# A decoder step on one core: sums over a head as two single-pass products of a split operand, and six instead of seven pairs of weight halves

## The chip, the core and the metric

The kernel runs on one core of a Trainium2 chip. The core has five engines that work side by side, each through its own list of instructions in a fixed order: TensorE (PE, matrix products into PSUM), VectorE (DVE), ScalarE (ACT), GpSimd (POOL) and SyncE (SP), which here issues the transfers. An instruction that waits holds back everything behind it on its engine. The metric is the time of one execution on the device in microseconds, the median of several runs.

## The reference

One layer of a hybrid decoder, for 256 prompt tokens and 8 decode tokens: 264 columns, with 2048 features each. A half-step FFN, a mixing stage with attention and RWKV-7 heads side by side, a second FFN, a final norm. What concerns the change are two sums over the 64 features of an RWKV head: the bonus, and the norm of each head's output.

```python
def swiglu(x, wg, wu, wd):
    return (jax.nn.silu(x @ wg) * (x @ wu)) @ wd
...
    S, y = wkv_scan(wkv0, r, logw, k, v, kk, a)
    mean = jnp.mean(y, axis=-1, keepdims=True)
    var = jnp.mean((y - mean) ** 2, axis=-1, keepdims=True)
```

The normalised y gets a weight and a bias per feature, then the bonus is added (the head's sum of r times k times a weight, times v), and the whole is multiplied by a gate. All inputs and outputs are float32.

## The kernel before

Activations lie features first: a tile is 128 features by 264 columns. A pair of RWKV heads fills the 128 rows, so there are eight pairs p = 0 to 7, in four batches of two.

**GEMMs.** A big product is made of single-pass matmuls (type float32r). Weight and activation are each split in two halves: hi, the value rounded by a cast, and lo, what is left. `gemm` (L143) does three matmuls per 128 features: hi by hi, hi by lo, lo by hi. Weights come from memory as raw tiles, four blocks of 128 wide; `chunk` (L125) casts one to hi on ScalarE (L136) and subtracts on VectorE to get lo (through `tt`, L58). A chunk so feeds 12 matmuls. NRAW = 7 raw buffers and NHL = 7 pairs of halves lie in rings. Small products use full fp32 operands.

**Stages.** The first FFN runs from 0 to about 700 us, the mixing stage to about 1107, the second FFN to the end. In the mixing stage 38 tiles of the input projection (`win`) are made one after another, then the output projection in three passes over the mixed tiles (`PASS`): tiles 0 to 3, then 8 to 11 with 4 and 5, then 6, 7 and 12 to 15. Tiles 0 to 7 are RWKV pairs, 8 to 15 attention.

**Order.** All that is not GEMM in the mixing stage is written as tasks, Python generators. `tick` takes each live task one step on, up to its next `yield`, and is called once a chunk of the GEMM. `pause(n)` lets n ticks go by, so that a product is written only when its operand has had time to be made. `drain` ticks without GEMM until the named tasks have ended. The order of each engine is settled when the program is built, from the written order, priorities and a modelled timeline. The tasks here are `prep` (one pair: decay, keys, bonus), `chain` (one batch: the scan over four chunks of 64 tokens, then `gnorm` per pair, then gate and `mixed[p]`), `attend` (one tile of attention), and `dec_load(p)` and `dec_attend(p)` (the decode tokens' attention, tiles 8 to 11 for p = 0 and 12 to 15 for p = 1). `dec_load(1)` begins only when the last batch's chain and `dec_attend(0)` have ended, and `dec_attend(1)` must end before pass 2 begins, since tiles 12 to 15 belong to it. The steps of `dec_attend`: scores, softmax, transposes (L871) and their copy out of PSUM (L872), products with the values, two multiply-adds, transposes back (L884), copies (L887, L889). Pass 2 then splits its tiles in halves (L939).

**The two sums.** C holds constants: `bo` is the block matrix of ones for two heads, `cm` the identity minus the mean over a head. The bonus product takes `rk` (280 columns: 264 and two columns for each of the 8 decode tokens). In `gnorm` the product with `cm` gives y minus its mean, and the one with `bo` on its square the variance:

```python
                yield from pause(PW[2])
                bps = mp()
                mm(bps[:, :T + 2 * NB], bo, rk)
...
                yp = mp()
                mm(yp[:, :T], cm, y)
                r = tmp()
                act(r, yp[:, :T], AF.Square)
                yield from pause(PW[3])
                vp = mp()
                mm(vp[:, :T], bo, r)
```

PW = (2, 1, 3, 2, 2) holds the lengths of the pauses. `chain` drives its batch's `gnorm` tasks for PW[3] + 1 = 3 ticks.

## Time and profile before

| | us |
|---|---|
| median of 3 runs | 1849.22 (1845.97 to 1851.04) |
| the profiled execution, a run of its own | 1846.21 |
| its span, first to last instruction | 1844.4 |
| granted TensorE clock, mean | 0.998 |
| first FFN, mixing, second FFN | about 700, 407, 737 |

Rows of the profile name an engine, a line of the kernel, an operation, the tile written and the tiles read, with shapes as partitions by elements. PEld is TensorE's loading of weights, which lies beside its products. A row of waits gives the engine that waits, the tile that it was to write, the engine and tile that it waited for, the total, the number and the longest wait. A row of the chain of waits gives a start, a length and the work in it. L58 and L61 are the lines of the helpers `tt` and `stt`, L74 that of `mm`.

### The profile page before, as it was taken

To read this page: it belongs to the slowest core of one execution; us is meant where nothing else is said; L and a number is where in the kernel's file an instruction comes from. 1 tells how busy PE (TensorE), PEld (TensorE's weight loads), DVE (VectorE), ACT (ScalarE), POOL (GpSimd) and SP (SyncE) were. 2 spreads that over 40 slices of the span, in tenths; PEclk is the share of its full clock that TensorE was granted. 3 is DMA by queue.
4 is the path that set the end of the run, shared out by engine and by line. 5 is a ranking of instruction groups with operands and counts; after the bars stand their busy time and mean duration, and the time that the engine had idled before them with its cause. 6 is when DMAs were issued, how large, how long until landed. Compare 5 with 4: busy or idle time off the path is not lost.

```text
span 1844.4 us, 46192 instructions
## 1 busy us (share of the span) xinstructions
PE 1821.4 (99%) x17212; PEld 1792.4 (97%) x17212; DVE 1311.4 (71%) x2613; ACT 1068.6 (58%) x2134; POOL 258.4 (14%) x389
## 2 busy tenths in 40 slices
PE   9999999999999999999998999999999999999998
PEld 9999999999999999998987899999999999999997
DVE  6966665656656577799888677876766676667765
ACT  6645555455554557777767766654545555455555
POOL 0401101010010122122111200220101001010012
PEclk9999999999999999999999999999999999999999
DMA  8666666666666677555666446666666666666664
GB/s 270 191 202 213 196 210 205 201 199 188 204 190 201 196 201 244 174 169 146 174 174 183 143 127 220 185 201 189 203 207 208 193 211 203 203 208 193 216 189 136
DMA packets 226465, 358.25 MB, mean 194 GB/s; under 512 B 38440, under 2 KB 82112, under 8 KB 226240
## 3 DMA queue, kind: packets, MB, share of 16 engines
q1 hardware_dynamic: 220352, 349.20, 62.9%
q10 hardware_dynamic: 5888, 6.11, 1.1%
q8 instruction: 135, 2.21, 0.5%
q14 instruction: 90, 0.74, 0.1%
HBM read 347.06 MB, written 10.22 MB: 194 GB/s over the span
## 4 chain that ended last, share of the span: by engine, by line
PE 91%; DVE 3%; DMA 3%; issue 1%; ACT 1%; POOL 0%; SPq 0%; POOLq 0%; ACTq 0%; DVEq 0%
PE acc L74 84%; PE m L74 6%; DVE lo L58 1%; DMA raw<-in_gu 1%; DMA raw<-in_win 0%; DVE Xt L58 0%; DVE st L58 0%; DMA X<-sa 0%; ACT hi L136 0%; DMA sa<-gm 0%; DMA out_vp<-s 0%; DVE t L61 0%; DMA s<-xsp 0%; DVE t L459 0%; DMA ld<-in_bias 0%
## 5 line engine op out<-in xcount | busy, mean ns | idle before, releaser
L58 DVE TENSOR_TENSOR lo<-raw,hi 128x512 fp32r<-128x512 f32 (+2 forms) x1312 | 876.5, 673 | 443.9 <-ACT hi L136 417.2
L136 ACT CAST hi<-raw 128x512 fp32r<-128x512 f32 (+2 forms) x1312 | 774.9, 596 | 665.0 <-PE acc L74 438.8
L74 PE MATMUL acc<-s,hi 128*128 128x264 f32 x5940 | 1030.6, 278 | 2.7 <-ACT s L939 1.2
L74 PEld LDWEIGHTS acc<-s,hi 128*128 128x128 f32 x5940 | 899.3, 189 | 9.4 <-ACT hi L136 2.2
L74 PE MATMUL acc<-s,lo 128*128 128x264 f32 x2970 | 824.2, 278 | 0.0
L74 PEld LDWEIGHTS acc<-s,lo 128*128 128x128 f32 x2970 | 561.8, 189 | 2.3 <-issue 0.9
L74 PE MATMUL acc<-t,hi 128*128 128x264 f32 x2752 | 465.0, 276 | 0.0
L74 PEld LDWEIGHTS acc<-t,hi 128*128 128x128 f32 x2752 | 414.9, 189 | 0.0
L74 PE MATMUL acc<-t,lo 128*128 128x264 f32 x1376 | 379.2, 276 | 0.0
L58 POOL TENSOR_TENSOR t<-t,t 128x264 f32<-128x264 f32 (+1 forms) x148 | 145.3, 981 | 1063.6 <-ACT hi L136 986.0
L74 PEld LDWEIGHTS acc<-t,lo 128*128 128x128 f32 x1376 | 260.1, 189 | 0.0
L74 PE MATMUL acc<-y,hi 128*128 128x264 f32 x648 | 113.8, 277 | 0.0
L74 PEld LDWEIGHTS acc<-y,hi 128*128 128x128 f32 x648 | 97.8, 189 | 0.2
L74 PE MATMUL acc<-y,lo 128*128 128x264 f32 x324 | 89.4, 276 | 0.0
L58 DVE TENSOR_TENSOR t<-acc,t 128x264 f32<-128x264 f32 x156 | 67.2, 431 | 20.6 <-PE acc L74 12.0
L58 POOL TENSOR_TENSOR o<-o,o 128x264 f32<-128x264 f32 x43 | 35.7, 829 | 195.8 <-ACT o L68 189.0
L74 PEld LDWEIGHTS acc<-y,lo 128*128 128x128 f32 x324 | 61.2, 189 | 0.0
L74 PE MATMUL acc<-o,hi 128*128 128x264 f32 x324 | 58.8, 276 | 0.0
L74 PEld LDWEIGHTS acc<-o,hi 128*128 128x128 f32 x324 | 48.8, 189 | 0.0
L61 DVE SCALAR_TENSOR_TENSOR s<-acc,s 128x264 f32<-128x264 f32 x96 | 40.9, 430 | 8.8 <-PE acc L74 6.3
L289 ACT CAST t<-t 128x264 fp32r<-128x264 f32 x86 | 38.3, 445 | 13.6 <-POOL t L58 8.1
L74 PE MATMUL m<-s,hi 128*128 128x264 f32 x260 | 44.8, 277 | 0.6 <-ACT hi L136 0.6
(246 smaller groups left out, 1266.5 us busy)
## 6 DMA issues: line engine op xcount, KB each, us to landing
raw<-in_gu SPq DMA_DIRECT2D x680, 256.0 KB, 3.4
raw<-in_dn SPq DMA_DIRECT2D x224, 256.0 KB, 3.0
raw<-in_win SPq DMA_DIRECT2D x152, 256.0 KB, 3.7
raw<-in_dn SPq DMA_DIRECT2D x160, 192.0 KB, 2.7
raw<-in_wout SPq DMA_DIRECT2D x48, 256.0 KB, 3.3
raw<-in_wout SPq DMA_DIRECT2D x32, 128.0 KB, 2.8
s<-xsp SPq DMA_DIRECT2D x16, 132.0 KB, 3.5
raw<-in_gu SPq DMA_DIRECT2D x16, 128.0 KB, 3.9
```

The costliest lines, as they stand in the source:

```text
L58: return e.tensor_tensor(out=out, in0=a, in1=b, op=op)
L61: return V.scalar_tensor_tensor(out=out, in0=a, scalar=s, in1=b, op0=op0, op1=op1)
L74: TE.matmul(out, lhsT, rhs, start=start, stop=stop, **k)
L136: A.copy(hi[:, :w], raw[:, :w])
L289: A.copy(halves(hi), pairs(u))
```

## The change

One hi/lo pair of weights is taken away (NHL = 6), and a ring of two pairs for activations is added (NHR = 2). `part` splits an operand: a cast on ScalarE, a subtract on VectorE. `whole` multiplies a constant matrix with both halves, in two single-pass matmuls that add up in PSUM. CR holds `bo` and `cm` in the single-pass type, cast once. No transfer is added or removed.

```diff
-CH, NRAW, NHL = 4, 7, 7
+CH, NRAW, NHL, NHR = 4, 7, 6, 2
...
+    def part(x, hl):
+        hi, lo = hl[:, 0], hl[:, 1]
+        x = pairs(x)
+        A.copy(halves(hi), x)
+        tt(V, halves(lo), x, halves(hi).bitcast(F32), ALU.subtract)
+        return hi, lo
+
+    def whole(o, w, xs, n):
+        for i, x in enumerate(xs):
+            mm(o[:, :n].rearrange("p (b a) -> p b a", a=2), w, woven(x), i == 0, i == len(xs) - 1)
...
+        CR = cp.tile([P, 2, P], F32R, name="CR")
...
+            def both(n):
+                return mx.tile([P, 2, T + 2 * NB], F32R, tag="hl", bufs=NHR, name=uid("hl"))[:, :, :n]
...
+            A.copy(CR.rearrange("p a b -> p (a b)"), C[:, CBO:CBO + 2 * P])
+            bor, cmr = CR[:, 0], CR[:, 1]
...
+                rks = part(rk, both(T + 2 * NB))
                 yield from pause(PW[2])
                 bps = mp()
-                mm(bps[:, :T + 2 * NB], bo, rk)
+                whole(bps, bor, rks, T + 2 * NB)
...
-                for _ in range(PW[3] + 1):
+                for _ in range(PW[3] + 3):
...
             def gnorm(y):
+                ys = part(y, both(T))
+                yield from pause(2)
                 yp = mp()
-                mm(yp[:, :T], cm, y)
+                whole(yp, cmr, ys, T)
                 r = tmp()
                 act(r, yp[:, :T], AF.Square)
+                rs = part(r, both(T))
                 yield from pause(PW[3])
                 vp = mp()
-                mm(vp[:, :T], bo, r)
+                whole(vp, bor, rs, T)
```

The change moves instructions at two places. The first is the start of pass 2 on PE, before the change. `acc` with `s` and `hi` or `lo` is the GEMM of w_out, L871 the transposes of the decode attention's probabilities, `uv,bk` its products with the values, L884 the transposes back:

```order
L74 MATMUL acc_17567<-s_17098,lo_17570 128x264
L871 MATMUL m_17049<-C,bk_16994 128x128 x2
L74 MATMUL acc_17567<-s_17102,hi_17587 128x264
...
L74 MATMUL acc_17599<-s_17106,lo_17620 128x264
L74 MATMUL m_17073<-uv_16919,bk_16994 32x128 x8
L74 MATMUL acc_17655<-s_17631,hi_17657 128x264
...
L74 MATMUL acc_17727<-s_17635,lo_17730 128x264
L884 MATMUL m_17129<-C,t_17082 128x128 x2
L74 MATMUL acc_17655<-s_17639,hi_17657 128x264
```

The same place on PE in the changed kernel, where the two lines of transposes are L892 and L905, and `s_17737` is the first half of tile 12:

```order
L74 MATMUL acc_17825<-s_17734,hi_17827 128x264
L74 MATMUL acc_17825<-s_17733,lo_17828 128x264
L892 MATMUL m_17211<-C,bk_17132 128x128 x2
L74 MATMUL m_17227<-uv_17057,bk_17132 32x128 x8
L905 MATMUL m_17259<-C,t_17236 128x128 x2
L74 MATMUL acc_17753<-s_17737,hi_17755 128x264
L74 MATMUL acc_17789<-s_17737,hi_17791 128x264
L74 MATMUL acc_17825<-s_17737,hi_17827 128x264
```

Before, 24 GEMM matmuls stood between the first and the second of the three steps and 18 between the second and the third; now none do. Between the scores and the first of them stood 87, now 69.

The second place is the bonus of the fifth pair. On VectorE before, `t_12744` is the operand `rk`, and the rows behind it are keys, the scan of other pairs (`Xt`), the token shift (`t` from `pj`) and a weight's low half:

```order
L61 SCALAR_TENSOR_TENSOR t_12744<-t_12177,vec,t_12666 128x264
L58 TENSOR_TENSOR bk_12775<-t_12666,t_12720 128x4x64
L58 TENSOR_TENSOR Xt_12612<-Xt_12612,st_12905 128x30
L61 SCALAR_TENSOR_TENSOR t_12629<-pj_10623,nmu,t_12629 128x264
L61 SCALAR_TENSOR_TENSOR t_12755<-pj_10621,nmu,t_12755 128x264
L58 TENSOR_TENSOR lo_13163<-raw_13161,hi_13162 128x512
```

On VectorE in the changed kernel, `t_12762` is the operand, and `hl_12817` holds its halves:

```order
L61 SCALAR_TENSOR_TENSOR t_12762<-t_12191,vec,t_12684 128x264
L58 TENSOR_TENSOR bk_12793<-t_12684,t_12738 128x4x64
L58 TENSOR_TENSOR st_12927<-X_12629,Xt_12630 128x30
L61 SCALAR_TENSOR_TENSOR t_12647<-pj_10625,nmu,t_12647 128x264
L58 TENSOR_TENSOR lo_13126<-raw_13124,hi_13125 128x512
L61 SCALAR_TENSOR_TENSOR t_12773<-pj_10623,nmu,t_12773 128x264
L58 TENSOR_TENSOR Xt_12630<-Xt_12630,st_12927 128x30
L58 TENSOR_TENSOR hl_12817<-t_12762,hl_12817 128x280
```

The subtract stands seventh behind the operand. On PE, in the changed kernel, `m_12874` is the bonus sum and the 64x2 products are those of the decode state:

```order
L74 MATMUL acc_12908<-s_10602,hi_13026 128x264
L74 MATMUL m_12874<-hl_12817,CR 128x280
L74 MATMUL m_12878<-XD,ld_12806 64x2 x2
L74 MATMUL m_12879<-XD,ld_12806 64x2 x2
L74 MATMUL m_12878<-XD,ld_12806 64x2 x2
L74 MATMUL m_12879<-XD,ld_12806 64x2 x2
L74 MATMUL m_12874<-hl_12817,CR 128x280
L74 MATMUL m_12878<-XD,ld_12808 64x2 x2
```

The one fp32 product has become two, with eight small products of the decode state between them, and the first stands seven GEMM matmuls later than the fp32 one did.

## The prediction

> **What bounds the kernel now.** I read the page's table of engines first, then a table of stretches, then what TensorE (PE) waits for, then the groups of instructions, and last the chain of waits.

> ```profile
> span 1844.4 us, 46192 instructions
> PE 1821.4 (99%) x17212; PEld 1792.4 (97%) x17212; DVE 1311.4 (71%) x2613; ACT 1068.6 (58%) x2134; POOL 258.4 (14%) x389
> 200.00:400.00 200.00, 200.00 (x1780) 200.00 (x1780) 127.49 (x216) 102.21 (x180) 19.74 (x19) 1.00 0.67 202
> 700.00:800.00 100.00, 99.72 (x977) 96.96 (x976) 78.76 (x158) 76.37 (x178) 22.12 (x60) 1.00 0.67 204
> 800.00:900.00 100.00, 97.30 (x1171) 92.17 (x1170) 88.26 (x257) 76.62 (x183) 22.03 (x62) 1.00 0.56 153
> 900.00:1000.00 100.00, 95.42 (x1319) 88.32 (x1318) 86.23 (x287) 69.60 (x178) 18.05 (x40) 1.00 0.60 170
> 1000.00:1110.00 110.00, 106.45 (x1143) 94.88 (x1142) 83.00 (x251) 76.15 (x210) 15.68 (x30) 0.98 0.51 152
> ```

> The windows read: stretch, length, busy PE, weight loads, VectorE, ScalarE, GpSimd, clock, DMA share, GB/s. The profiled run took 1846.2 us, 1.8 around its span, 3.0 under the median. In the first FFN (200 to 400) PE is never idle. In the mixing stage, 700 to 1110, PE still sets the time, but VectorE is busy 86 to 88 us of 100 between 800 and 1000. What PE waits for there (total, times, longest):

> ```profile
> PE m L74 <- DVE Xt L58: 3.2, 3, 1.6
> PE m L74 <- DVE st L58: 2.0, 1, 2.0
> PE acc L74 <- ACT s L939: 1.2, 1, 1.2
> PE m L74 <- DVE mxv L796: 1.0, 1, 1.0
> PE m L74 <- ACT t L809: 1.0, 1, 1.0
> PE m L74 <- ACT t L68: 0.8, 1, 0.8
> PE m L805 <- DVE t L810: 0.5, 1, 0.5
> PE m L74 <- DVE gm L58: 0.5, 2, 0.3
> ```

> With a few shorter ones it waits 11 us of 410; the five rows on VectorE (Xt, st, mxv, t at L810, gm) make 7.2, and a shorter one 0.2 more. So a microsecond less on PE is a microsecond less of time, unless a wait takes its place, and only VectorE is near enough to make one.

> **What PE saves.** The changed products are 8 of 280 columns (bonus) and 16 of 264 (mean and variance in `gnorm`).

> ```profile
> L74 PE MATMUL m<-t,C 128*128 128x264 f32 x32 | 9.8, 392 | 0.8 <-ACT t L68 0.8
> L74 PE MATMUL m<-t,C 128*128 128x280 f32 x16 | 5.3, 412 | 0.0
> L74 PE MATMUL m<-y,C 128*128 128x264 f32 x16 | 4.6, 392 | 0.0
> 63.19 639.13 PE acc L74 x5681
> 940.34 0.89 PE m L74 x4
> ```

> Each fp32 product has two records (of the 32, half belong to the norm sum `nps`, which stays). The records overlap, so price comes from the chain: two mean products, four records, take 0.89 us, or 446 ns each; 5681 single-pass matmuls of the GEMMs take 639.13, or 112.5 ns each. Two single-pass ones cost 225, so 221 ns go, 16 times: 3.5 us. By columns, 280/264, the bonus falls from 473 to 239: 8 x 234 = 1.9. PE saves **5.4 us**. This is an upper bound: where a product ends a wait anyhow, its shortening is worth nothing.

> **What the split adds.** Each operand costs a cast on ScalarE and a subtract on VectorE; pass 0 and 1 of w_out have such pairs on equal shapes:

> ```profile
> L939 ACT CAST s<-y 128x264 fp32r<-128x264 f32 x8 | 3.3, 438 | 0.9 <-DVE y L61 0.9
> 1102.05 1.47 DVE L58 TENSOR_TENSOR s<-o,s 128x264 fp32r<-128x264 f32 x4 [2.09 <-ACT s L939]
> ```

> Casts: 24 x 0.44 = 10.6 us, beside ScalarE's 70 to 76 us of 100, so hidden by PE. Subtracts: four in a row last 1.47, so 0.36 each and 24 x 0.36 = 8.7. Sixteen of them fall between 840 and 1010, where VectorE is nearly full. If all of that surfaced it would cost 16 x 0.36 = 5.8; the other end is that the new order removes the 7.4 us that PE waits on VectorE. Neither end is excluded. I take a value near the present waits, because 8.7 us is only 2% more over the stage, and let them grow by a tenth: **+0.8**. The one cast of the constants, 128x256, stands ahead of the stage's work: nothing.

> **The start of pass 2.** Here the order counts most. Pass 2 needs the last decode attention, which is loaded only after the last batch's chain. That chain now has two more ticks, so the attention's last three steps no longer stand among the matmuls of pass 1 but one behind another. Before:

> ```profile
> 1084.97 9.98 PE acc L74 x87
> 1094.96 0.22 PE m L871 x2
> 1093.68 0.62 POOL L65 TENSOR_SCALAR bk<-bk,stb 128x129 f32<-128x129 f32 x1 [24.48 <-ACT hi L136]
> 1095.21 0.37 ACT L872 COPY bk<-m 128x256 f32<-128x256 f32 x1
> 1095.18 2.70 PE acc L74 x24
> 1097.88 0.57 PE m L74 x16
> 1099.36 0.60 DVE L61 SCALAR_TENSOR_TENSOR t<-bk,bk,m 128x128 f32<-128x128 f32 x2
> 1098.45 2.22 PE acc L74 x18
> 1100.68 0.23 PE m L884 x2
> ```

> The scores ended at 1084.97; softmax was ready at 1093.68 + 0.62 = 1094.30, 9.33 us later; 87 GEMM matmuls lay between, so the transposes (L871) waited for nothing. Now 69 lie there, 69 x 0.1125 = 7.76: PE waits 9.33 - 7.76 = 1.6, and up to 3.7 if three more weight subtracts (0.70 each, in the groups below) come ahead of the softmax's VectorE steps; I take 2.0, near the lower. Behind the transposes the copy (0.37, and 0.05 of hand-over) lay under 24 matmuls and the two multiply-adds (0.60 and 0.1) under 18; now nothing lies there: 1.1 more. The last wait, 1.2 for the cast at L939, was open before and stays. What is late next is the mixed columns' split, already in that 1.2. Together **+3.1** (from 1.1, if the softmax is early, to 4.8).

> **The bonus.** Its second product reads the low half, and that waits for a subtract which, for the fifth pair, stands seventh behind the operand in VectorE's new order.

> ```profile
> 839.23 0.49 DVE L61 SCALAR_TENSOR_TENSOR t<-t,vec,t 128x264 f32<-128x264 f32 x1
> 839.63 0.42 DVE L58 TENSOR_TENSOR bk<-t,t 128x256 f32<-128x256 f32 x1
> 839.97 0.20 DVE L58 TENSOR_TENSOR Xt<-Xt,st 128x30 f32<-128x30 f32 x1
> 840.10 0.48 DVE L61 SCALAR_TENSOR_TENSOR t<-pj,nmu,t 128x264 f32<-128x264 f32 x1
> 840.34 0.40 PE L74 MATMUL m<-t,C 128*128 128x280 f32 x1
> 905.54 0.49 DVE L61 SCALAR_TENSOR_TENSOR t<-t,vec,t 128x264 f32<-128x264 f32 x1
> 906.62 0.64 PE L74 MATMUL m<-t,C 128*128 128x280 f32 x2
> ```

> For the fifth pair the operand was ready at 839.72 and PE came at 840.34, 0.62 later. In the new order PE comes seven matmuls later (0.79), reaches the low half after one product (0.12) and eight small decode ones (the rows above had 16 such in 0.57, so 0.29): 1.8 us after the operand. VectorE has six instructions first: bk (0.42), two of Xt's kind (0.20), two of t's (0.48) and a weight subtract (0.70), then the split's own 0.43: 2.9, less 0.08 for each of seven hand-overs (839.23 to 839.63 is 0.40 for a row of 0.49), so 2.4 and a wait of 0.6. The seventh pair (905.54) had 0.59 and now has two rows more ahead on VectorE, a weight subtract among them, 3.3 against 1.8: 1.5. The other pairs had a microsecond or more to spare. That makes 2.1 at most and 0 if PE arrives late for another reason; the middle, near **+1.1**. Behind the waiting product on PE stand the small decode products and the GEMM, so the wait is whole.

> `gnorm`'s own two splits lie under the added pause and the old one, some 18 matmuls or 2.0 us each, against 0.44 + 0.43 and a short queue: nothing; without that cover, 0.87 us twice a batch, 7 us in all.

> **One buffer pair fewer.** A chunk is twelve matmuls, 12 x 0.1125 = 1.35 us; seven pairs give PE's readiness a lead of 9.5 us, six give 8.1.

> ```profile
> L136 ACT CAST hi<-raw 128x512 fp32r<-128x512 f32 x1104 | 677.8, 617 | 561.5 <-PE acc L74 404.2 <-DVE lo L58 116.8 <-issue 8.6
> L58 DVE TENSOR_TENSOR lo<-raw,hi 128x512 fp32r<-128x512 f32 x1104 | 765.3, 697 | 362.2 <-ACT hi L136 336.6 <-PE acc L74 0.9
> ```

> Cast and subtract take 0.62 + 0.70, so 6.7 us of the 8.1 are spare. The casts' idle time is mostly for PE to free a buffer (404 us of 562): the engines run ahead, and PE does not starve. I take **nothing**, with bounds of 0 and +1.4, one chunk, for a place like 800 to 1000 where VectorE's backlog may have eaten the lead.

> **The sum.** -5.4 + 3.1 + 1.1 + 0.8 + 0 = -0.4, on the profiled 1846.2: 1845.8. The median lies 3.0 above the profiled run, so 1848.8, say **1849.0**. The terms' bounds, not all at one end, make it 1845 to 1853.5.

> **Rivals.** *The saving arrives whole (faster).* PE is the busiest engine, and what it no longer does comes off: no new wait forms because VectorE reaches each subtract before PE needs it. Then 1849.2 - 5.4 = 1843.8, and lower if the old waits on VectorE shrink, to 1836 if all 7.4 go. For it: PE is 95 to 100% busy everywhere. Against it: PE's waits in this stage are on VectorE, which gets the work, and the three steps at pass 2 do stand together in the new order. [...] Chance 0.20.

> *VectorE decides from 840 to 1010 (slower).* If it has no idle time there that matters, the 16 subtracts surface, 16 x 0.36 = +5.8; PE's saving counts only outside, for the first four bonuses (0.94) and the last batch's four head norms (0.88), -1.8; with pass 2's +3.1 the sum is +7.1: 1856.3. It decides from the point where PE's waits on VectorE pass 7.4 + 5.8 = 13 us. For it: 86 to 88 of 100 busy. Against: even there PE waits for it less than 5 us in 100. Chance 0.17.

> *The buffers bind (slower).* The twelve parts of the FFNs each end with a burst of evictions on VectorE; if each lost one chunk's lead, 12 x 1.35 = 16 us, less 5: about 1860. Against: no PE wait in the window 200 to 400. Chance 0.04.

> *The change does not do what it says (slower).* If a pass with the copied constants is no cheaper than half the fp32 product, nothing is saved, and the rest stays: +5.0, 1854.2. The single-pass GEMM price speaks against it. Chance 0.04.

> **How the numbers follow.** The forecast has 0.55. A difference of 0.3%, 5.5 us, is about what a measurement of this kernel can tell from no change. Faster than that are about six tenths of the first rival and a sliver of the forecast: 0.15. Slower are most of the VectorE rival, the buffers, half of the last, and a tail of the forecast: 0.23. The rest is 0.62. The range runs from 1842 (the saving whole and some of the waits gone) to 1857.5 (just over the VectorE rival); beyond it lie some 0.07 below and 0.09 above. The forecast's own is 1845 to 1853.5.

> **What would show it.** Right: in the changed profile the products of the split operands with the constants appear at 112 to 120 ns in the chain; PE's wait at the head of pass 2 is some 4 us instead of 1.2, put down to the transposes, the copy, the multiply-adds and the cast; PE waits on a subtract's output ahead of the fifth and seventh bonus; its waits on VectorE in 700 to 1110 sum to 8 to 10; none in the first FFN. Wrong: waits on VectorE beyond 13 us (the VectorE rival), PE waits for weight halves in an FFN (the buffers), waits under 7 in all (the saving arrives whole), or a product of two passes that takes over 300 ns.

## The result: 0.68% slower, and where the profile shows it

The changed kernel took 1860.8 us (median of 4 runs, 1857.35 to 1862.72) against 1848.9 before: ratio 1.0068, 95% interval 1.0053 to 1.0084, so 10 to 16 us slower. The profiled run's span is 1857.5 us against 1844.4, 13.1 more. The page's first part, and then the windows of the mixing stage, columns as before:

```profile
span 1857.5 us, 46196 instructions
PE 1828.4 (98%) x17212; PEld 1798.4 (97%) x17212; DVE 1309.2 (70%) x2637; ACT 1070.7 (58%) x2157; POOL 251.4 (14%) x389
```

```profile
700.00:800.00 100.00, 99.52 (x968) 96.76 (x967) 79.66 (x161) 77.17 (x180) 20.91 (x60) 1.00 0.68 203
800.00:900.00 100.00, 96.05 (x1160) 91.09 (x1159) 86.60 (x251) 77.76 (x189) 21.09 (x61) 1.00 0.54 150
900.00:1000.00 100.00, 91.94 (x1270) 85.50 (x1269) 86.05 (x285) 63.58 (x162) 15.05 (x38) 0.97 0.57 159
1000.00:1110.00 110.00, 105.99 (x1116) 93.14 (x1115) 84.58 (x261) 77.05 (x222) 18.97 (x30) 0.99 0.54 156
1110.00:1200.00 90.00, 87.91 (x768) 87.05 (x769) 66.21 (x126) 53.71 (x106) 6.74 (x11) 0.97 0.60 182
```

Both FFNs are unchanged. The GEMM matmuls can be counted in both traces, and the same ones compared: those from 6200 to 8620, the mixing stage, took 408.0 us before and 422.2 now; the others differ only by 1.1 us at the very start, in the changed kernel's favour. VectorE and ScalarE are hardly busier in the windows than before. What changed is PE: less busy between 900 and 1000, and its clock below 1 there and in the last window, from 1110, where it was full before. What PE waits for from 700 to 1125:

```profile
PE m L74 <- DVE kr L58: 3.6, 1, 3.6
PE m L74 <- DVE Xt L58: 2.3, 2, 1.9
PE m L74 <- DVE hl L58: 1.9, 2, 1.6
PE m L74 <- DVE st L58: 1.8, 1, 1.8
PE m L74 <- ACT t L68: 1.3, 2, 1.0
PE acc L74 <- DVE s L58: 1.3, 2, 0.9
PE acc L74 <- ACT s L960: 1.2, 1, 1.2
PE m L74 <- ACT hl L88: 1.0, 1, 1.0
```

All waits of the stage sum to 18.6 us against 11.1. The rows for hl are the bonus's halves, but for 0.3 us of a head norm's. The products themselves became as short as worked out:

```profile
884.47 0.72 PE L74 MATMUL m<-hl,CR 128*128 128x264 f32 x4
```

These are two head norms' mean products, both passes of each; the single rows of the trace end 0.113 us apart.

The largest single wait, on the keys kr, stands at the third batch's solve. SP's and VectorE's rows say why:

```profile
941.81 0.55 SPq L616 DMA_DIRECT2D sb<-Xt  x1
942.46 0.56 SPq L146 DMA_DIRECT2D raw<-in_win  x1
944.69 0.87 SPq L621 DMA_DIRECT2D TT<-sb  x2
946.09 0.93 SPq L621 DMA_DIRECT2D TT<-sb  x2
...
949.35 0.43 DVE L627 STREAM_TRANSPOSE TN<-TT 32x256 f32<-32x256 f32 x1 [2.30 <-DMA TT<-sb]
949.82 0.69 DVE L58 TENSOR_TENSOR lo<-raw,hi 128x512 fp32r<-128x512 f32 x1
950.43 0.42 DVE L61 SCALAR_TENSOR_TENSOR kr<-t,t 128x256 f32<-128x256 f32 x1
950.76 0.42 DVE L58 TENSOR_TENSOR kr<-t,t 128x256 f32<-128x256 f32 x1
951.33 1.14 PE L74 MATMUL m<-kr,bk 64*128 64x128 f32 x4 [3.60 <-DVE kr L58]
```

The solve's result left 6 to 7 us later than before (its last transfer was issued at 941.8, and at 935.3 before), while VectorE's transpose of what comes back stands at the same GEMM matmul (7690) as before: VectorE stood still twice for 2.3 us, with the keys behind it. And then the clock, in windows of 2 us (PE busy is the second figure, the clock the third from the end):

```profile
946.00:948.00 2.00, 1.72 (x15) 1.53 (x14) 0.43 (x1) 1.47 (x7) 0.00 (x0) 1.00 0.61 122
948.00:950.00 2.00, 0.00 (x0) 0.00 (x0) 0.62 (x2) 0.00 (x0) 0.00 (x0) 1.00 0.89 242
950.00:952.00 2.00, 0.67 (x4) 0.70 (x5) 2.00 (x7) 0.17 (x2) 0.00 (x0) 0.75 0.34 125
952.00:954.00 2.00, 2.00 (x17) 1.78 (x16) 1.86 (x7) 0.77 (x2) 0.00 (x0) 0.50 0.81 236
954.00:956.00 2.00, 2.00 (x10) 2.00 (x10) 1.00 (x2) 0.80 (x3) 0.00 (x0) 0.50 0.50 125
```

After the wait PE ran at half its clock from 951.0 to 957.8, two stretches of 3.41 us. Such stretches stand in the mixing stage four times here (two there, and at 1108.0 and 1114.8) and once before (1014.3); PE worked 12.9 us of them here and 3.4 before. In the stretch of before the GEMM matmuls end 0.220 us apart, at the full clock of the first FFN 0.112 (300 to 320), so half of the difference, 4.7 us, is lost to the clock. The other executions agree: their mean granted clock is 0.9935 for the changed kernel (4 of them) and 0.9962 for the kernel before (113, with those beside the experiments), and 0.27% of 1859 us is 5.0 us. The balance of the stage by these traces: products -5.4, waits +7.5, clock +4.7, which is +6.8 of +14.2. The other 7.4 us is in matmuls that show no wait and yet end later than the ones before them allow, around waits and between small products of other kinds; the records don't say more.

### The profile page after: what moved, and what is told of

Same layout as the page of the kernel before. It is cut to its first block, busy times and chain, and to the rows that moved or that the text cites. A ratio compares the mean times of both kernels' runs of the same rounds, so it can differ in the third digit from the quotient of the medians.

```text
span 1857.5 us, 46196 instructions
## 1 busy us (share of the span) xinstructions
PE 1828.4 (98%) x17212; PEld 1798.4 (97%) x17212; DVE 1309.2 (70%) x2637; ACT 1070.7 (58%) x2157; POOL 251.4 (14%) x389
## 4 chain that ended last, share of the span: by engine, by line
PE 88%; DVE 4%; DMA 3%; ACT 2%; issue 2%; POOL 0%; SPq 0%; POOLq 0%; DVEq 0%; ACTq 0%
PE acc L74 82%; PE m L74 6%; DVE lo L58 2%; DMA raw<-in_win 1%; ACT hi L147 1%; DVE st L58 0%; DMA sb<-Xt 0%; DVE Xt L58 0%; ACT L68 0%; ACT t L68 0%; DMA raw<-in_wout 0%; DVE t L61 0%; DMA raw<-in_gu 0%; DVE s L58 0%; DVE t L763 0%
## 5 line engine op out<-in xcount | busy, mean ns | idle before, releaser
L58 DVE TENSOR_TENSOR lo<-raw,hi 128x512 fp32r<-128x512 f32 (+2 forms) x1312 | 878.4, 675 | 452.4 <-ACT hi L147 435.1
L74 PE MATMUL acc<-s,hi 128*128 128x264 f32 x5940 | 1034.3, 278 | 2.9 <-DVE s L58 1.3
L74 PEld LDWEIGHTS acc<-s,hi 128*128 128x128 f32 x5940 | 901.9, 190 | 9.2 <-ACT hi L147 2.0
L74 PE MATMUL acc<-s,lo 128*128 128x264 f32 x2970 | 824.8, 278 | 0.5 <-DVE lo L58 0.4
L74 PEld LDWEIGHTS acc<-s,lo 128*128 128x128 f32 x2970 | 563.1, 190 | 4.4 <-issue 1.9
L74 PE MATMUL acc<-t,hi 128*128 128x264 f32 x2752 | 465.0, 276 | 0.0
L74 PEld LDWEIGHTS acc<-t,hi 128*128 128x128 f32 x2752 | 414.9, 189 | 0.0
L74 PE MATMUL acc<-t,lo 128*128 128x264 f32 x1376 | 378.7, 276 | 0.0
L58 POOL TENSOR_TENSOR t<-t,t 128x264 f32<-128x264 f32 (+1 forms) x148 | 140.2, 947 | 1065.9 <-ACT hi L147 986.6
L74 PEld LDWEIGHTS acc<-t,lo 128*128 128x128 f32 x1376 | 260.1, 189 | 0.0
L74 PE MATMUL acc<-y,hi 128*128 128x264 f32 x648 | 113.8, 277 | 0.0
L74 PEld LDWEIGHTS acc<-y,hi 128*128 128x128 f32 x648 | 97.8, 189 | 0.2
L74 PE MATMUL acc<-y,lo 128*128 128x264 f32 x324 | 89.4, 276 | 0.0
L58 DVE TENSOR_TENSOR t<-acc,t 128x264 f32<-128x264 f32 x156 | 67.2, 431 | 15.9 <-PE acc L74 6.0
L58 POOL TENSOR_TENSOR o<-o,o 128x264 f32<-128x264 f32 x43 | 34.8, 808 | 199.7 <-ACT o L68 192.4
L74 PEld LDWEIGHTS acc<-y,lo 128*128 128x128 f32 x324 | 61.2, 189 | 0.0
L74 PE MATMUL acc<-o,hi 128*128 128x264 f32 x324 | 58.8, 276 | 0.0
L74 PEld LDWEIGHTS acc<-o,hi 128*128 128x128 f32 x324 | 48.8, 189 | 0.0
L61 DVE SCALAR_TENSOR_TENSOR s<-acc,s 128x264 f32<-128x264 f32 x96 | 40.6, 427 | 11.3 <-PE acc L74 9.6
L74 PE MATMUL m<-s,hi 128*128 128x264 f32 x260 | 44.8, 277 | 0.0
L74 PE MATMUL acc<-o,lo 128*128 128x264 f32 x162 | 44.7, 276 | 0.0
```

What stands on the lines that cost most here:

```text
L58: return e.tensor_tensor(out=out, in0=a, in1=b, op=op)
L61: return V.scalar_tensor_tensor(out=out, in0=a, scalar=s, in1=b, op0=op0, op1=op1)
L74: TE.matmul(out, lhsT, rhs, start=start, stop=stop, **k)
```

## The experiments

Eighteen kernels. Ratios are to the kernel before on the same chip, and 0.1% is 1.85 us. Each theory is explained in the expectation that first names it. First: which part, and which place.

**Six pairs of weight halves alone.**

```diff
-CH, NRAW, NHL = 4, 7, 7
+CH, NRAW, NHL = 4, 7, 6
```

> The kernel before with six pairs of weight halves instead of seven, nothing else. Two-places theory (the loss sits where the third batch's triangular solve reaches its DMA, 930 to 970 us, and at the start of pass 2, and has nothing to do with the buffers): within 0.15% of the kernel before, no wait of PE in the first FFN, pass 2 starts with the one wait of 1.2 us. Buffers theory: +8 to +12 us, with waits of PE on weight halves (hi or lo). VectorE theory (the subtracts' busy time surfaces): no change.

Ratio 0.9995 (0.9986 to 1.0004). The buffers cost nothing.

**The bonus alone.**

```diff
 # of the changed kernel
-                for _ in range(PW[3] + 3):
+                for _ in range(PW[3] + 1):
 # and gnorm as before
```

> The change with its head norms left as they were before (fp32 products, three ticks); bonus split and six pairs stay. Two-places theory: pass 2 starts as before with one wait of about 1.2 us; at the third batch's solve VectorE waits for the TT transfers less than the changed kernel's 4.6 us, since the solve stands 19 and not 33 GEMM matmuls later than before; PE's waits for hl of about 2.5 us stay; together +1 to +4 us on the kernel before. Buffers theory: +8 to +12. VectorE theory (0.36 us a subtract, eight of 24, and each surfaces): +1 to +3, spread over all eight and not in one place.

Ratio 1.0001 (0.9992 to 1.0009): the 1.9 us that the products save do not show.

```profile
PE m L74 <- ACT hl L88: 2.8, 2, 1.8
PE m L74 <- DVE hl L58: 1.2, 1, 1.2
```

PE waits 1.0 and 1.2 us for the bonus's halves. The 1.8 is the wait of a product of the scan (m<-N,PT) that reads no half; it is put down to a cast of the split on ScalarE. Other waits went in return: all of the stage's sum to 11.5 us, against 11.1 before. So the waits alone don't say where the saving went.

**The head norms alone.**

```diff
-                rks = part(rk, both(T + 2 * NB))
...
-                whole(bps, bor, rks, T + 2 * NB)
+                mm(bps[:, :T + 2 * NB], bo, rk)
```

> The change with its bonus left as it was before (one fp32 product); head norms split and six pairs stay. Two-places theory: the start of pass 2 loses 6 to 7 us against the kernel before, at waits on the decode attention's three steps and a halved TensorE clock behind them, the solve loses 0 to 3, the products save 3.5: +3 to +6 us in all. Buffers theory: +8 to +12. VectorE theory: 16 subtracts surface, 5.8 less 3.5, so +2, spread over four batches, and pass 2's start costs under 3.

Ratio 1.0047 (1.0035 to 1.0059), 6.5 to 11 us more: above the 3 to 6 of the two-places theory.

**The last decode attention loaded earlier**, when the last batch's sweep over its four chunks has ended.

```diff
+                bt.swept = True
                 g2s = [load(I["g2"][bt.p0 + k], (P, P)) for k in range(n)]
...
-                            spawn(dec_load(1, [bat[-1], d]))
+                            spawn(dec_load(1, [spawn(swept(bts[-1])), d]))
```

> The changed kernel with one edit: the last decode attention is loaded when the last batch's sweep has ended, and not five ticks later when its norm and gate have. PE's order is that of the changed kernel up to 8352 GEMM matmuls; then the attention's three last steps stand at 8454, 8472 and 8499 and not all at 8514. Two-places theory: the waits and the two halved-clock stretches at the start of pass 2 go, 5 to 8 us less than the changed kernel (1853 to 1856), while the loss at 930 to 970 stays at about 7. Buffers theory and VectorE theory: within 1.5 us of the changed kernel.

Ratio 1.0029 (1.0019 to 1.0039), 1853.2 us, as the two-places theory said. At the start of pass 2, PE's waits in the changed kernel (from 1100 to 1125), and then with the earlier load (1080 to 1125):

```profile
PE acc L74 <- ACT s L960: 1.2, 1, 1.2
PE acc L74 <- DVE s L58: 0.9, 1, 0.9
PE m L905 <- DVE t L61: 0.5, 1, 0.5
PE m L74 <- ACT bk L893: 0.5, 1, 0.5
```

```profile
PE acc L74 <- DVE s L58: 1.2, 3, 0.6
PE m L897 <- ACT bk L799: 0.4, 1, 0.4
```

Neither of the two halved-clock stretches at that place is left; the profile has five others, earlier in the stage, but over the executions the granted clock is 0.9958 on average, against the changed kernel's 0.9935. So the start of pass 2 cost the change some 7 us (0.39% between the two ratios), and 5 us lie elsewhere.

Next: what moved the attention, and whether the waits at the solve and the bonus can be shifted away.

**The splits without the norms' added ticks.**

```diff
                 ys = part(y, both(T))
-                yield from pause(2)
...
-                for _ in range(PW[3] + 3):
+                for _ in range(PW[3] + 1):
```

> The changed kernel without the two added ticks of the head norms (no pause before the mean product, three ticks as before); the splits stay. Two-ticks theory (the prediction's: the added ticks alone push the decode attention to the head of pass 2): the loss there goes, 6 to 8 us less than the changed kernel's 1860.8. Late-sweep theory (the last batch's sweep itself comes later, 36 of the 60 matmuls by which the scores moved, because the splits lengthen what leads to it): the scores stand at 8471, later than the changed kernel's 8445, all three steps still behind one another at 8514, so the loss there stays, and the norms' products wait for their halves, 1 to 3 us: 1859 to 1864.

Ratio 1.0148 (1.0134 to 1.0163), far worse than either theory said. The steps stayed behind one another, and the norms' products waited for their halves, one of them 3.8 us; 30.7 us of the stage were at half clock. The ticks are needed; they were not what moved the attention.

**The solve's result used two ticks later**, on top of the earlier load.

```diff
-DWAIT, RWAIT = (10, 9, 8, 8), (12, 11, 9, 10)
+DWAIT, RWAIT = (10, 9, 8, 8), (12, 11, 11, 12)
```

> The earlier decode load (as in the run before it) and two more ticks between the solve's transfers and their use for the third and fourth batch (RWAIT 11 and 12 instead of 9 and 10). Solve theory (VectorE, held by two transposes until the TT transfers land, holds the keys for which PE waits 3.6 us, and the clock halves behind): VectorE's waits for TT fall from 6.9 us to under 1, the wait for kr goes, 3 to 7 us less than with the early load alone: 1846 to 1850. Backlog theory (VectorE is late in any case, the transfer is only where it shows): the wait comes back on another tile of VectorE, within 1.5 us of the early load alone, 1852 to 1855.

Ratio 1.0059 (1.0046 to 1.0071), by the ratios 5.5 us worse than with the earlier load alone, which neither theory said. VectorE's hold for TT shrank only from 4.3 to 2.8 us and PE's longest wait for kr from 3.0 to 1.8, and other waits came in their place:

```profile
PE m L827 <- ACT o L841: 1.9, 1, 1.9
PE m L74 <- DVE Xt L58: 1.9, 1, 1.9
PE m L74 <- DVE kr L58: 1.8, 1, 1.8
PE m L74 <- DVE st L58: 1.8, 1, 1.8
PE m L74 <- DVE hl L58: 1.6, 1, 1.6
PE m L827 <- DVE kr L58: 1.5, 1, 1.5
```

**The bonus's products one tick later**, on top of that.

```diff
-PW = (2, 1, 3, 2, 2)
+PW = (2, 1, 4, 2, 2)
```

> The last kernel with one more tick between the bonus's split and its products (PW[2] = 4). If PE's waits for the bonus's halves are lateness of one subtract: the 2.6 us for hl go, 1.5 to 3 us less than the kernel with the later solve, 1844 to 1848, and below the kernel before. If they are VectorE's backlog: the wait is found again ahead of the next product that VectorE feeds, and the time stays within 1 us.

Ratio 1.0025 (1.0016 to 1.0035): 6 us less than the kernel with the later solve, more than either theory said, but no better than the earlier load alone (1.0029), and not below the kernel before. The waits for hl were still 4.3 us: 2.1 for the bonus, and 2.2 now for a head norm's product. So the two moves together bring nothing. The solve theory found no support, though the hold was shortened only in part, and why one more tick took back 6 us is not shown. A backlog on the engines that feed PE is left as the guess.

**The kernel before with the earlier load**, as a control (the edit as above).

> The kernel before with the earlier decode load alone, as a control. Two-places theory: it had only 1.2 us of wait at the start of pass 2, so 0 to 1.5 us less than the kernel before. If the early load is a gain of its own, independent of the change: 5 to 8 us less.

Ratio 0.9999 (0.9991 to 1.0008). The earlier load helps only where the change had done harm.

Then: is it the added work, or the waiting for it?

**The load alone.** The splits are made, and the products stay as they were.

```diff
-                rks = part(rk, both(T + 2 * NB))
+                part(rk, both(T + 2 * NB))
...
-                whole(bps, bor, rks, T + 2 * NB)
+                mm(bps[:, :T + 2 * NB], bo, rk)
 # the same in gnorm, with three ticks
```

> All 24 casts and subtracts of the change are made, with six weight pairs, but nothing reads them: the products stay single fp32 ones, the head norms keep three ticks. So VectorE and ScalarE carry the change's whole load, PE saves nothing, and no product waits for a half. Load theory (VectorE is full from 840 to 1010, so the added 8.7 us of subtracts make PE wait): 4 to 9 us more than the kernel before, and waits of PE on VectorE of 11 to 16 us. Latency theory (the cost comes from products that stand behind their halves, and from what that moves): within 2 us of the kernel before.

Ratio 1.0029 (1.0019 to 1.0039), 3.5 to 7 us for work that nothing reads. But PE's waits did not grow: 11.4 us in all, against 11.1 before. Single ones grew, the longest from 2.0 to 2.6 us, and 17.1 us of the stage were at half clock instead of 3.4 in the profile of before. Over the executions the granted clock fell from 0.9964 to 0.9946 on average, which is 3.3 us of 1850: here the load is paid largely through the clock.

**The subtracts on GpSimd**, with the earlier load.

```diff
-        tt(V, halves(lo), x, halves(hi).bitcast(F32), ALU.subtract)
+        tt(G, halves(lo), x, halves(hi).bitcast(F32), ALU.subtract)
```

> The changed kernel with the earlier decode load, and with the splits' subtract on GpSimd (14% busy) instead of VectorE. Load theory: VectorE is back at its work of before, 3 to 6 us less than with the early load alone, 1847 to 1850. Latency theory: each half comes later still (GpSimd's additions of this shape take 0.8 to 1.1 us against 0.43), no gain or 1 to 5 us more, 1853 to 1858, and waits for hl above 2.6 us.

Ratio 1.0066 (1.0052 to 1.0080), 7 us worse than on VectorE, and more than the 1 to 5 of the latency theory. PE's waits for the halves grew from 2.6 to 3.4 us, and its wait for kr from 3.0 to 4.7. Taking the subtracts off VectorE did not pay.

**The head norms with the earlier load** (the third and the fourth edit together).

> Head norms split, bonus as before, six pairs, with the earlier decode load. If pass 2's start carries nearly all that the norms cost: 5 to 7 us less than the norms alone, 0 to 3 us above the kernel before. If the norms' loss is spread over the batches: 3 us or more remain above the kernel before.

Ratio 1.0023 (1.0014 to 1.0032), 4.4 us less than without the earlier load; 4 us remain above the kernel before, so the norms' loss is spread over the batches as well as at pass 2.

**Splits only where PE did not wait before**, with the earlier load (`gnorm` is that of before, `gnorm2` the changed one).

```diff
+                rks = part(rk, both(T + 2 * NB)) if p < 4 else None
...
+                late = bt.i == len(BATCH) - 1
+                gs = [(gnorm2 if late else gnorm)(Ys[k]) for k in range(n)]
+                for _ in range(PW[3] + (3 if late else 1)):
```

> Splits only where PE never waits: the bonus of the first four pairs and the head norms of the last batch, with the earlier decode load; the rest as before. PE saves 4 x 0.234 + 4 x 0.221 = 1.8 us, and up to the 1.2 us of wait at the start of pass 2 goes. By all theories nothing is added at 840 to 1010: 1 to 3 us less than the kernel before.

Ratio 1.0005 (0.9996 to 1.0014), a miss: even the 1.8 us don't show. No version here beat the kernel before while computing the same.

Last: each cost by itself.

**The saving alone.** The instructions that make the operands write them in the single-pass type, and both passes read them. The kernel leaves out the low halves and counts the high ones twice, so it times the products and does not compute the layer.

```diff
+                rkr = tmp((P, T + 2 * NB), F32R)
...
-                rks = part(rk, both(T + 2 * NB))
...
+                whole(bps, bor, [rkr] * 2, T + 2 * NB)
 # the same in gnorm, with three ticks
```

> The 24 products as two single-pass ones, but without any split: each operand is written in the single-pass type by the instruction that makes it, and both passes read it (so the lows are left out and the his counted twice, and columns of the sums stand in another order); six weight pairs, the head norms' ticks as before. PE saves 5.4 us, nothing is added on VectorE or ScalarE, no product waits for a half. Saving theory (PE bounds the stage): 4 to 6 us less than the kernel before, 1842 to 1844. If the saving only turns into longer waits: within 1.5 us of the kernel before.

Ratio 0.9975 (0.9965 to 0.9986): 4.6 us less, 2.6 to 6.5, which fits the 5.4.

**Saving and load together.** The same, with every `part` called and its result left.

> The same, with the 24 casts and subtracts made and read by nothing. If saving and load add up (-5.4 and +5.2): within 2 us of the kernel before, and the rest of the changed kernel's loss is lateness of the halves and the start of pass 2. If the load costs more where PE is faster: 2 to 6 us more than the kernel before.

Ratio 1.0017 (1.0008 to 1.0026). The load costs 7.8 us here (0.42% between the two), more than the products save. It is not paid through the clock this time: both profiles have 10.2 us at half clock, and the means over the executions are 0.9954 and 0.9952. PE's waits rose instead, from 11.1 to 15.7 us.

**The two added ticks alone**, in the kernel before.

```diff
-                for _ in range(PW[3] + 1):
+                for _ in range(PW[3] + 3):
...
             def gnorm(y):
+                yield from pause(2)
```

> The kernel before with the head norms' two added ticks and nothing else. Two-ticks theory of the prediction (they push the decode attention to the head of pass 2): 2 to 7 us more, with waits there. Late-sweep theory: the scores stand at 8309 GEMM matmuls and the three steps at 8404, 8428 and 8452, among the matmuls of pass 1, so nothing is lost there, and the time is within 1.5 us of the kernel before.

Ratio 1.0021 (1.0012 to 1.0030). Both theories missed: the ticks cost 4 us, but not at pass 2, where no such wait is seen; they cost it in the middle of the stage, where PE now waits 2.5 us for N and 2.1 for XD between 925 and 950, and the one wait of before was 1.6. All waits of the stage sum to 12.3 us against 11.1, so waits alone don't make up the 4.

**One pass.** As the saving alone, with `[rkr] * 1`; it too leaves out the low halves.

> As the saving alone, but with one single-pass product each, of operands rounded by their producers (the lows are left out, and columns of the sums stand in another order). PE saves 16 x 0.334 + 8 x 0.354 = 8.2 us. Saving theory: 6 to 9 us less than the kernel before, 1839 to 1842. If shorter products only turn into longer waits: 0 to 3 less.

Ratio 0.9975 (0.9964 to 0.9985), the same as with two passes, and between what the two theories said. The second half of the shortening, 2.8 us by the price of a pass, does not show; the two intervals, each 2 us to either side, just leave room for it.

**The casts alone, and the subtracts alone**, edits of the kernel with the load alone.

```diff
 # casts alone: in part
-        tt(V, halves(lo), x, halves(hi).bitcast(F32), ALU.subtract)
 # subtracts alone: in part
-        A.copy(halves(hi), x)
-        tt(V, halves(lo), x, halves(hi).bitcast(F32), ALU.subtract)
+        tt(V, halves(lo), x, x, ALU.subtract)
```

> As the load alone (single fp32 products, six pairs, three ticks), but only the 24 casts on ScalarE are made; the subtracts are left out. If VectorE is the engine whose load costs (86 to 88% busy at 800 to 1000): within 1.5 us of the kernel before. If ScalarE's share costs as well (each cast stands ahead of the chain's copies): 2 to 5 us more.

> As the load alone, but only the 24 subtracts on VectorE are made (of the operand from itself, so that they wait for no cast); the casts are left out. If VectorE is the engine whose load costs: 3 to 7 us more than the kernel before. If ScalarE's: within 1.5 us.

Casts 1.0033 (1.0022 to 1.0044), 6 us; subtracts 1.0013 (1.0004 to 1.0022), 2.4 us, between what the two theories said. The two don't add up to the load alone (5.4 us). It is ScalarE's share that costs most, against the theory I had held from the start.

An edit can also change the order that is settled when the program is built. The casts alone hardly do: against six pairs alone, some 30 of VectorE's 2613 instructions stand elsewhere and 5 of ScalarE's, and no step on PE moves by more than 10 GEMM matmuls. With the subtracts alone some 490 of VectorE's move, and steps on PE by up to 66. So the 6 us are the price of the casts themselves, and the 2.4 us hold a change of order too.

How a cast of 0.44 us comes to cost more shows at the sixth pair's bonus. ScalarE with the casts alone, and VectorE and PE behind it:

```profile
861.37 0.46 ACT L88 CAST hl<-t 128x280 fp32r<-128x280 f32 x1 [1.64 <-POOL t L58]
861.86 0.48 ACT L674 COPY W<-m 128x384 f32<-128x384 f32 x1
865.19 0.69 DVE L58 TENSOR_TENSOR lo<-raw,hi 128x512 fp32r<-128x512 f32 x1 [1.63 <-ACT hi L146]
869.02 0.27 PE L74 MATMUL m<-N,PT 64*64 64x64 f32 x2 [1.92 <-DVE Xt L58]
```

The same copy and the same product with six pairs alone:

```profile
859.00 0.48 ACT L657 COPY W<-m 128x384 f32<-128x384 f32 x1
866.55 0.27 PE L74 MATMUL m<-N,PT 64*64 64x64 f32 x2 [1.07 <-DVE Xt L58]
```

The cast waits 1.64 us for GpSimd, which makes the operand's last 16 columns, and everything behind it on ScalarE waits with it: ahead of the cast ScalarE's rows stand 0.75 us later than with six pairs alone, behind it 2.86. A weight's cast is among them. VectorE waits 1.63 us for that one, and PE for VectorE, 1.92 instead of 1.07. From 872.1 PE then runs one stretch at half clock. Counted by GEMM matmuls, it falls back by 3.2 us between 861 and 873. The row of waits names VectorE; what held it was ScalarE, and behind that GpSimd.

A second place, from 923 to 933, takes 2.7 more; later 3.0 come back, where the kernel with six pairs has a halved stretch of its own (979.4). PE's waits at the second place, from 925 to 940, with six pairs alone, then with the casts, and the windows of the latter:

```profile
PE m L74 <- DVE Xt L58: 1.6, 1, 1.6
```

```profile
PE m L74 <- DVE N L58: 2.6, 1, 2.6
```

```profile
932.00:937.00 5.00, 2.35 (x35) 2.12 (x33) 5.00 (x18) 2.10 (x5) 1.48 (x5) 1.00 0.56 171
936.00:941.00 5.00, 4.90 (x42) 4.87 (x43) 3.67 (x14) 3.04 (x9) 0.31 (x3) 0.66 0.36 115
```

The wait grew by 1.0 us, and the clock behind it was halved for one stretch, which the shorter wait had not brought about: 1.7 us more. The holds for GpSimd are longer in the changed kernel, 5.9 us in all, where the casts alone have 2.2:

```profile
ACT hl L88 <- POOL t L58: 5.9, 5, 3.4
```

Before, PE alone read this operand, later. What the changed kernel would take without these holds was not tried.

## Why the prediction was wrong

The forecast was 1849.0 (1842.0 to 1857.5), the time 1860.8. By its steps:

1. **PE saves 5.4 us: right.** The products run at 112 to 120 ns a pass, and alone they bring 4.6 us. One pass instead of two brought nothing more that shows.
2. **"Casts: 24 x 0.44 = 10.6 us, beside ScalarE's 70 to 76 us of 100, so hidden by PE": this step failed first, and by most.** It put the casts at nothing; casts that nothing reads cost 6 us. With the casts alone, the sixth pair's cast waited 1.64 us for GpSimd, and ScalarE's rows stood 2.86 us later behind it, against 0.75 ahead of it: weights' casts, and copies of the scan, for which VectorE and then PE waited. I did not ask what a cast itself waits for, nor what is queued behind it, and a mean share of 70% did not show it.
3. **Subtracts, +0.8: mis-sized.** They measured 2.4 alone; casts and subtracts together 5.4 without the saving and 7.8 with it. I let PE's waits on VectorE grow by a tenth, to 8 to 10 us; from 700 to 1110 they came to 13.0, which was my border to the VectorE rival. With the load alone the waits' sum did not grow, and the clock fell; beside the saving the waits grew by 4.6 us, and the clock did not fall. The clock was in my windows (0.98 between 1000 and 1110) and in no term of the sum. The profile that I read was also a mild one: its clock of 0.998 is that of 10 of the 113 executions of the kernel before, whose mean is 0.9962.
4. **The start of pass 2, +3.1: the place was right, the size and the cause were not.** It measured about 7. PE's waits there rose from 1.2 to 3.1 us, near the forecast, though the wait of 2.0 for the softmax did not come and a late VectorE took its place; two stretches at half clock, some 3.2 us, came on top. The other 2 us are not accounted for. The cause I gave, "that chain now has two more ticks", falls: alone, the ticks leave the steps among pass 1's matmuls; without them, the splits still push them to its end. The order shows the last sweep itself 36 GEMM matmuls later, of the 60 by which the scores moved. The other 24 lie between the sweep and the scores, 93 GEMM matmuls instead of 69; but these are 119 with the splits and no added ticks, and 59 with the ticks alone, so the ticks don't explain them. Why the splits move the sweep and the scores stays open.
5. **The bonus, +1.1: the places were right, the size was at its upper bound, and for the fifth pair the step was another.** PE waited 1.6 us for the seventh pair's low half, against 1.5 worked out. For the fifth pair it waited 1.0, against 0.6, but ahead of the first product, for the cast, and not for the subtract:

```profile
841.75 0.44 ACT L88 CAST hl<-t 128x280 fp32r<-128x280 f32 x1 [3.35 <-POOL t L58]
842.24 0.39 PE L74 MATMUL m<-hl,CR 128*128 128x280 f32 x1 [0.99 <-ACT hl L88]
```

   That the number came near there is luck. Alone, the bonus's split brings nothing of the 1.9 us it saves.
6. **The norms' own splits, nothing: nearly right.** PE's waits for their halves are 0.3 us, thanks to the ticks: without them, one alone was 3.8. But the ticks cost 4 us alone, and were priced only at pass 2.
7. **The buffers, nothing: right.** The rival that put the time at 1860 came nearest in number and was wrong in cause.

In a chain of differences: saving alone -4.6, its load +7.8, halves that are read with their ticks +2.2 (the earlier load's kernel less saving and load), the start of pass 2 +7.2, together +12.6. They add up because each is the step from one kernel to the next, and each carries some 2.5 us of uncertainty, so the +2.2 can't be told from nothing. The VectorE rival, 1856.3, was the nearest in mechanism; it left out ScalarE and the clock.

## What to carry to other kernels

Before moving work from a busy engine to two that look idle, ask of each added instruction what it waits for, what stands behind it in its engine's list, and whether that engine feeds a chain which the busy engine waits for; a share of 70% was no cover here. Price a wait on TensorE not by its length alone but by whether the clock is halved behind it, as it was here for 6.83 us behind the 3.60 us for kr. And make the cheap test first: the added work with nothing reading it, and the saving with nothing added. Here these two kernels (+5.4 and -4.6) already said that there was nothing to win, though not how much would be lost.

## What the runs showed of the hardware

In the mixing stage the halved clock came in stretches of 3.41 us or whole multiples of it: one of 3.413 in the profile of before, from 1014.29, and 6.827, 3.413 and 3.413 in that of the changed kernel, from 950.99, 1108.01 and 1114.83, the later two 46 and 48 steps of 3.413 from the first. In each of the 20 profiles the starts there lie whole multiples of that apart. Cut into such steps from 700 to 1150 us, each by its own starts, all 20 traces give these counts, by how long PE was idle in a stretch, and how many of the stretches were followed by one at half clock:

```
PE idle in a stretch of 3.41 us    stretches    followed by half clock
2.0 us and more                        16               16
1.5 to 2.0                             34               22
1.0 to 1.5                             66               21
0.5 to 1.0                             75                9
under 0.5                            2442               11
```

So a wait can cost its own length in one execution, and with one halved stretch 1.7 us more in the next, half of 3.41 by my estimate: the kernel with six pairs alone, whose waits sum to those of before within 0.2 us, had three halved stretches in its profile where the kernel before had one. The spread of one kernel's runs, some 6 us, goes with the clock: of the 113 executions of the kernel before that stand beside the experiments, the 13 with a granted clock of 0.994 took 1850.1 us on average, and the 10 with 0.998 took 1845.9.
